# Where the gate of w_out is multiplied in: from the weights to the output projection's product

## The chip, the cores and the metric

The kernel runs on one core of a Trainium2 chip. Five engines of that core matter here: TensorE (PE in the profile; PEld is its loading of weights), VectorE (DVE), ScalarE (ACT), GpSimd (POOL) and SyncE (SP), which issues nearly all DMA transfers. Each engine works off its own queue in order, and instructions of different engines wait for each other on semaphores. The metric is the device time of one execution in microseconds (us).

## The reference, cut to what matters

One layer of a diffusion backbone works on a sequence of 2048 latent tokens of 1024 channels (`x`). Six vectors of 1024 numbers come from the conditioning vector `c`; one of them, `g1`, is the gate of the first residual addition:

```
h = modulate(rmsnorm(x, norm_mix), sh1, sc1)
o = token_mixers(h @ w_in, ...)          # (2048, 1024): recurrence heads and gMLP heads
x = x + g1 * (o @ w_out)                 # the output projection, gated, added
h2 = modulate(rmsnorm(x, norm_ffn), sh2, sc2)
x = x + g2 * conv_ffn(h2, w_up, conv_w, conv_b, w_down)
out = rmsnorm(x, norm_final)
```

`g1` has one number for each of the 1024 output columns. So `g1 * (o @ w_out)` is the same as `o @ (w_out * g1)`, with the columns of `w_out` scaled.

## The kernel before, in words

**Matmuls in three parts.** Every large product is made of float32r matmuls. An operand is split into a rounded high part and the rest (`split`, L131: a cast on ACT, L133, and a subtraction, L134, on the engine that is passed, POOL if none), and `mm3` (L136) adds up high by high, high by low and low by high. In the profile L65 is every matmul, L69 every transpose on TensorE.

**Two halves of the sequence, heads in turn.** The first and longest part (to about 978 us) runs the input projection for the two halves of 1024 tokens. `run_banks` (L524) walks over blocks of 128 columns of `w_in`; each block's weights are loaded into one of three raw tiles of 4 KB per partition (`raw_tile`, L214) and split by ACT and DVE. Between the blocks' matmuls the work of the recurrence is spread out: `hg` (L791) for one head and half, with sums over columns of `kh` and `kl` (L798, L800), levels of scores and `mi` banks for transposes and states; `sgu` (L678) for the gMLP heads, with the normalised tile `nt` (L709).

**Due times.** This spread-out work consists of Python generators in two lists, `hg_q` and `bg_q`. `slot()` (L185) is called after every three matmuls; a generator goes on once the modelled time of TensorE has advanced by the number that it last yielded, in us. So `yield 5.0` in a background step means: the next piece is put into the queues 5.0 us of matmul time later. Behind that a planner orders the instructions of each engine, by when it reckons that each can start; instructions under `pin` stay in the program's order.

**w_out in the background.** `w_out_ops` (L982) is one generator of `bg_q`, between the blocks that make the six vectors (`ada_block`, L951, which also stores `g1` and `g2` in `g_d`) and the taps and `w_down_ops` (L999). For each of the 8 blocks of 128 rows and each of the 2 halves of 512 columns it takes a raw tile, loads the half row into its left half (L989) and the gate, broadcast to 128 partitions, into its right half (L990); 5.0 us later it multiplies on DVE (L993), splits into `wo_hi` and the tile's right half (L994), stores both into `wo_d` (L995, L996), and 2.5 us later begins the next. `wo_hi` has the tag `acc`, with one buffer. `w_down_ops` loads whole raw tiles (L1007), multiplies them by `g2` 9.0 us later (L1009) and stores them (L1010).

**The output projection.** From 978 to 1168 us, `wo` is in SBUF (13 loads, L916 and L1145) and TensorE works through 16 tiles of 128 tokens (L1334). For tile t the code asks for tile t+2's operand (`fetch_o`, L1317) and tile t+1's rows of `x` (`fetch_x`, L1327), splits tile t+1's operand (`split_o`), and multiplies into `pd`, a PSUM tile of two banks of 512 columns, first the one bank, then the other (48 matmuls). There are two such tiles in turn. DVE adds the rows of `x` (L1358, giving `xn`), SP stores `xn` (L1359), and ACT squares it and sums the squares (L1360). After every second tile `second_norm` (L1275) makes the reciprocal roots on POOL (L126, L128), scales the two tiles on DVE (L1279), and then, in four steps, transposes them on TensorE, applies `a2` and `s2` (L1292) and splits the result (L1295 to L1305). Its transposes are put into the queue as background: the first `first` = 6.0 us of matmul time behind the pair's end, the others 3.0 us apart. For the last pair these are 9.0 and 4.5.

**Then** the up-projection, the convolution and the down-projection follow, to the end of the span. `a_tiles` (L1196) gives the split weights of the up-projection; its tags `Ah` and `Al` have four buffers each, of 2 KB per partition, and three of the four pairs are filled while the output projection ends.

Of the kernel before, what the change touches and what calls it, by code (L numbers as in the profile page):

```python
# [9 lines left out]
F32 = mybir.dt.float32  # L10
F32R = mybir.dt.float32r
# [7 lines left out]
P = 128  # L19
# [14 lines left out]
AL = 512  # L34
# [49 lines left out]
def tile_trunk(ctx, tc, x, c, cx, c_ctx, w_ada, b_ada, norm_mix, norm_ffn, w_in, hg_norm, sgu_g, sgu_b,  # L84
               w_sp, b_sp, w_out, w_up, conv_w, conv_b, w_down, norm_final, masks, out):
    nc = tc.nc
    V, S, G, T = nc.vector, nc.scalar, nc.gpsimd, Tensor(nc.tensor)
    ld = nc.sync.dma_start
    st = nc.sync.dma_start
# [3 lines left out]
    w_ada, w_in, w_out, w_up, w_down = w_ada[0], w_in[0], w_out[0], w_up[0], w_down[0]  # L93
# [21 lines left out]
    g_d = dr.tile([2, D], F32, name="g_d")  # L115
# [3 lines left out]
    wo_d = dr.tile([P, NK, 2, D], F32, name="wo_d")  # L119
# [11 lines left out]
    def split(hi, lo, raw, eng=None, keep=lambda i: i):  # L131

        keep(S.copy(hi, raw))  # L133
        (eng or G).tensor_sub(lo, raw, hi.bitcast(F32))  # L134

    def mm3(ps, lhi, llo, rhi, rlo, first, last):  # L136
        T.matmul(ps, lhi, rhi, start=first, stop=False)
        T.matmul(ps, lhi, rlo, start=False, stop=False)
        T.matmul(ps, llo, rhi, start=False, stop=last)
# [51 lines left out]
    with es1:  # L191
# [22 lines left out]
        def raw_tile():  # L214
            return p1.tile([P, D], F32, tag="raw", name="raw", bufs=3)
# [766 lines left out]
        def w_out_ops():  # L982

            for k in range(NK):
                for n in range(2):
                    cl = slice(n * 512, n * 512 + 512)
                    raw = raw_tile()
                    w, g = raw[:, :512], raw[:, 512:]
                    ld(w, w_out[k * P:(k + 1) * P, cl])  # L989
                    ld(g, g_d[0:1, cl].broadcast_to([P, 512]))  # L990
                    yield 5.0
                    hi = pm.tile([P, 512], F32, tag="acc", name="wo_hi")
                    V.tensor_mul(w, w, g)  # L993
                    split(hi.bitcast(F32R), g.bitcast(F32R), w, V)  # L994
                    st(wo_d[:, k, 0, cl], hi)  # L995
                    st(wo_d[:, k, 1, cl], g)  # L996
                    yield 2.5

        def w_down_ops():  # L999

# [174 lines left out]
    px = esx.enter_context(tc.tile_pool(name="px", bufs=1, reuse_waits="tile"))  # L1175
# [10 lines left out]
    def zbank():  # L1186
        return ps2.tile([P, 512], F32, tag="uz", name="uz", bufs=2)
# [5 lines left out]
    def dbank():  # L1193
        return ps2.tile([P, 2, 512], F32, tag="dn", name="dn", bufs=2)
# [4 lines left out]
    def v_tile():  # L1199
        return px.tile([P, TH + GW], F32, tag="cv", name="cv", bufs=3)  # L1200
# [4 lines left out]
    def raw_tile2(j):  # L1205
        return px.tile([P, 4, 2 * P], F32, tag=f"raw{j}", name="raw")


    class Unit:
# [15 lines left out]
        def prep(self, i):  # L1225

            a11, a21 = self.raw[0][:, :, :P], self.raw[0][:, :, P:]
            a12, a22 = (self.raw[1][:, :, :P], self.raw[1][:, :, P:]) if i else (None, None)
            self.A[i] = a_tiles()
            hi, lo = self.A[i]  # L1230

            if i == 1:
                self.s2 = (c_tile()[:, :4, :].bitcast(F32) if self.slots[0] == 1 else
                           px.tile([P, 4, P], F32, tag="s1", name="s2"))
            split(hi, lo, (a11, a12, self.s2, a11, a21, a12, a22)[i])
            if i == 0:
                G.tensor_sub(a21, a11, a21)
            elif i == 1:
                pin(G.tensor_sub(self.s2, a22, a21))
            elif i == 2:  # L1240
                G.tensor_add(a11, self.s2, a11)
            elif i == 3:
                G.tensor_sub(a12, a12, self.s2)  # L1243
# [30 lines left out]
    with tc.tile_pool(name="po", bufs=1, reuse_waits="tile") as po:  # L1274
# [39 lines left out]
        def fetch_o(t):  # L1314
            hh, g = tiles[t]
            raw = raw_tile2(2 * (t % 2 == 0)).rearrange("p a b -> p (a b)").rearrange("p (k c) -> p k c", c=P)
            ld(raw, oT_d[hh][:, :, g * P:(g + 1) * P])  # L1317
            return raw

        def split_o(t, raw):  # L1320
            o = po.tile([P, 2, NK, P], F32R, tag="o", name="o", align_bytes=AL) if t % 2 else first_o[0]()
            split(o[:, 0], o[:, 1], raw, V, pin)
            return o

        def fetch_x(t):
            xt = raw_tile2(2 if t == nt_ - 1 else 1 + 2 * (t % 2))
            ld(xt.rearrange("p a b -> p (a b)"), x[t * P:(t + 1) * P, :])  # L1327
            return xt.rearrange("p a b -> p (a b)")

        raw_o = {1: fetch_o(1)}  # L1330
        xts = {0: fetch_x(0)}
        ops = {0: first_o[1]}
        xs = []
        for t, (hh, g) in enumerate(tiles):  # L1334
            if g % 2 == 0:
                ss = px.tile([P, 2], F32, tag="ss", name="ss", bufs=2)
            if t + 2 < nt_:
                raw_o[t + 2] = fetch_o(t + 2)
            if t + 1 < nt_:
                ops[t + 1] = split_o(t + 1, raw_o.pop(t + 1))  # L1340
                xts[t + 1] = fetch_x(t + 1)
            if t + 2 == nt_:
                units[0].load()
            if t + 1 == nt_:
                units[1].load_half(0)
            pd = dbank()
            o = ops.pop(t)
            for n in range(2):
                for k in range(NK):
                    mm3(pd[:, n, :], o[:, 0, k, :], o[:, 1, k, :], wo[k][:, 0, n * 512:(n + 1) * 512],  # L1350
                        wo[k][:, 1, n * 512:(n + 1) * 512], k == 0, k == NK - 1)
                    if t + 1 < nt_ or n == 0 and k < 4:
                        bg_q.slot()
            if t + 1 == nt_:
                for n in range(3):
                    prep(n)
            xn = v_tile()[:, :D]
            V.tensor_add(xn, pd.rearrange("p a b -> p (a b)"), xts.pop(t))  # L1358
            st(xn_d[t], xn)  # L1359
            S.activation(pd.rearrange("p a b -> p (a b)"), xn, AF.Square, accum_out=ss[:, g % 2:g % 2 + 1])  # L1360
            if t + 1 == nt_:
                units[1].load_half(1)
            xs.append(xn)
            if g % 2:
                how = (ubank, 6.0, 3.0) if t + 1 < nt_ else (lambda: dbank()[:, 0, :], 9.0, 4.5)
                norm = second_norm(hh, g - 1, xs, ss, *how)
                if t + 1 < nt_:
                    bg_q.drain()
                wait = next(norm)
                bg_q.drain()  # L1370
                bg_q.add(norm)
                bg_q.at = T.t + wait
                xs = []
# [193 lines left out]
    for n, (u, i) in enumerate(prods):  # L1567
# [10 lines left out]
        p = zbank() if i == 1 else u.z if i in (4, 6) else u.x  # L1578
        hi, lo = u.A[i]
# [40 lines left out]
    V = Kept(nc.vector, pin)  # L1620
# [111 lines left out]
    xts, odd_ss = {}, {}  # L1732
# [131 lines left out]
```

## Time and profile before

| | before |
|---|---|
| median of 3 runs | 2441.85 us (2439.68 to 2443.75) |
| the profiled execution | 2441.35 us, span 2439.6 us |
| TensorE busy | 2403.6 us (99% of the span) |
| DVE / ACT / POOL busy | 1669.5 / 1039.4 / 882.7 us |
| moved by SP's queue | 397.28 MB |
| 368 to 504 us, where w_out is rounded: TensorE / DVE / ACT busy of 136 | 131.58 / 83.00 / 60.81 us |
| 978 to 1168 us, the output projection: TensorE / DVE / ACT busy of 190 | 188.70 / 104.71 / 86.07 us |

How it is read: a row of the profile's groups names the line, the engine, the operation, what is written and read (`out<-in`), the shapes and the count; behind the bar stand the busy time, the mean duration in ns, and the time that the engine stood idle just before these instructions, with what ended most of it. In a timeline a row has the start, the duration, and in brackets the idle time before it. A table of stretches gives each engine's busy time (with the instructions), the clock that TensorE was granted as a share of full speed, the share of the DMA engines' time and the GB/s.

### The profile page before, as it was taken

The numbers are of one execution on the slowest core, as the hardware profiler recorded it, in microseconds if no ns is written. First come the engines' busy times: TensorE is split into PE (matmuls) and PEld (weight loads), VectorE is DVE, ScalarE is ACT, GpSimd is POOL, SyncE is SP. The second block draws the span as 40 slices with busy tenths as digits, with TensorE's granted clock in tenths as the row PEclk, the third lists the DMA queues.
The fourth block names the chain that finished last, engine by engine and source line by source line (L and its number), as shares of the span: only waits on it lengthen the run. The fifth ranks groups of instructions, "written<-read, shape, count | busy, mean of one in ns | idle before, by whom it ended". The sixth has DMA issues, their size and how long they took to land.

```text
span 2439.6 us, 32382 instructions
## 1 busy us (share of the span) xinstructions
PE 2403.6 (99%) x11711; PEld 1995.0 (82%) x11711; DVE 1669.5 (68%) x2293; ACT 1039.4 (43%) x1802; POOL 882.7 (36%) x796
## 2 busy tenths in 40 slices
PE   8999999999999999999999999999999999999998
PEld 5887887888888887788888888888888887888887
DVE  5867795756776786465596666639866772776875
ACT  4554334434444443354554444434445442332343
POOL 1232110110121132000688778787888870000002
PEclk9999999999999999999999999999999999999999
DMA  8365446573354323768922322562222238934745
GB/s 311 108 209 163 152 136 196 193 241 121 113 177 156 104 104 141 239 209 260 309 82 86 97 81 91 183 230 97 86 94 86 88 112 334 324 121 147 229 153 196
DMA packets 307853, 400.10 MB, mean 164 GB/s; under 512 B 33113, under 2 KB 216161, under 8 KB 304621
## 3 DMA queue, kind: packets, MB, share of 16 engines
q1 hardware_dynamic: 304404, 397.28, 48.3%
q8 instruction: 92, 1.51, 0.2%
q10 hardware_dynamic: 3289, 0.76, 0.1%
q14 instruction: 68, 0.56, 0.1%
HBM read 288.85 MB, written 109.13 MB: 163 GB/s over the span
## 4 chain that ended last, share of the span: by engine, by line
PE 47%; issue 2%; POOL 1%; DVE 1%; ACT 1%; SPq 0%; DMA 0%; POOLq 0%; ACTq 0%
PE ux L65 19%; PE uz L65 14%; PE dn L65 14%; POOL ra L1723 0%; POOL rr L1724 0%; DVE dn L1434 0%; POOL Al L134 0%; ACT mhl L133 0%; ACT jk L1715 0%; DVE odd L80 0%; ACT odd L1793 0%; DVE mhl L80 0%; DVE thl L80 0%; ACT thl L133 0%; POOL raw L1243 0%
## 5 line engine op out<-in xcount | busy, mean ns | idle before, releaser
L1434 DVE SCALAR_TENSOR_TENSOR dn<-gp,taps,dn 128x1024 f32<-128x1024 f32 x352 | 448.3, 1285 | 97.2 <-ACT dn L1431 92.8
L65 PE MATMUL dn<-thl,mhl 128*128 128x512 f32 x1680 | 381.5, 389 | 1.2 <-ACT thl L133 1.2
L65 PEld LDWEIGHTS dn<-thl,mhl 128*128 128x128 f32 x1680 | 315.1, 188 | 67.6 <-ACT thl L133 2.1
L134 POOL TENSOR_TENSOR Al<-raw,Ah 128x512 fp32r<-128x512 f32 x264 | 341.3, 1309 | 69.3 <-ACT Ah L133 40.5
L65 PE MATMUL pj<-xh,whi 128*128 128x512 f32 x896 | 362.4, 405 | 0.0
L65 PE MATMUL pj<-xl,whi 128*128 128x512 f32 x896 | 351.3, 392 | 0.6 <-POOL xl L134 0.6
L65 PE MATMUL pj<-xh,wlo 128*128 128x512 f32 x896 | 350.9, 392 | 0.9 <-DVE wlo L134 0.9
L133 ACT CAST Ah<-raw 128x512 fp32r<-128x512 f32 x264 | 163.0, 620 | 240.4 <-PE ux L65 134.6
L65 PE MATMUL ux<-xah,Ah 128*128 128x512 f32 x528 | 205.7, 390 | 0.3 <-ACT keep L1498 0.3
L65 PEld LDWEIGHTS pj<-xh,wlo 128*128 128x128 f32 x896 | 168.4, 188 | 36.9 <-DVE wlo L134 1.1
L65 PEld LDWEIGHTS pj<-xh,whi 128*128 128x128 f32 x896 | 168.9, 189 | 33.7 <-issue 3.5
L65 PEld LDWEIGHTS pj<-xl,whi 128*128 128x128 f32 x896 | 169.1, 189 | 31.9 <-POOL xl L134 1.5
L65 PE MATMUL dn<-wo,o 128*128 128x512 f32 x768 | 182.9, 394 | 1.7 <-DVE nt L717 0.9
L65 PE MATMUL uz<-yf,Ah 128*128 128x512 f32 x704 | 174.0, 389 | 0.0
L590 POOL TENSOR_TENSOR K<-K,tot 128x512 f32<-128x512 f32 x40 | 58.3, 1458 | 303.8 <-DVE tot L520 158.0
L65 PEld LDWEIGHTS dn<-wo,o 128*128 128x128 f32 x768 | 142.0, 188 | 31.6 <-issue 1.1
L65 PE MATMUL ux<-yf,Ah 128*128 128x512 f32 x528 | 155.4, 389 | 0.0
L65 PEld LDWEIGHTS uz<-yf,Ah 128*128 128x128 f32 x704 | 132.1, 188 | 27.4
L65 PE MATMUL ux<-xah,Al 128*128 128x512 f32 x528 | 141.7, 390 | 1.0 <-POOL Al L134 1.0
L65 PE MATMUL ux<-xal,Ah 128*128 128x512 f32 x352 | 137.1, 389 | 0.0
L1723 POOL TENSOR_SCALAR ra<-ss 128x1 f32<-128x1 f32 x8 | 5.3, 662 | 360.4 <-ACT jk L1715 360.4
L134 DVE TENSOR_TENSOR wlo<-raw,whi 128x1024 fp32r<-128x1024 f32 x68 | 85.1, 1252 | 72.6 <-ACT whi L133 70.7
(345 smaller groups left out, 4480.5 us busy)
## 6 DMA issues: line engine op xcount, KB each, us to landing
raw<-in_w_up_dram SPq DMA_DIRECT2D x88, 512.0 KB
mr<-m SPq DMA_DIRECT2D x85, 512.0 KB
raw<-in_w_in_dram SPq DMA_DIRECT2D x68, 512.0 KB
sT<-wd SPq DMA_DIRECT2D x88, 256.0 KB
raw<-in_w_ada_dram SPq DMA_DIRECT2D x32, 512.0 KB
yf<-yd SPq DMA_DIRECT2D x14, 1024.0 KB
m<-cv SPq DMA_DIRECT2D x22, 544.0 KB
raw<-in_w_down_dram SPq DMA_DIRECT2D x22, 512.0 KB
```

The costliest lines, as they stand in the source:

```text
L65: return self.engine.matmul(out, lhsT, rhs, **kw)
L133: keep(S.copy(hi, raw))
L134: (eng or G).tensor_sub(lo, raw, hi.bitcast(F32))
L590: e.tensor_mul(view(K2, row * W + o, src), view(K, o, src), view(tot, t0, [[4, n], [ts, 2], [0, B]]))
L1434: V.scalar_tensor_tensor(out=cr, in0=gt[:, t // 3:t // 3 + RH, t % 3:t % 3 + GW], scalar=taps[:, t * NF + f:t * NF + f + 1], in1=cr, op0=A ...
L1723: G.tensor_scalar(out=a, in0=ss, scalar1=plus, scalar2=None, op0=ALU.add)
```

## The change

The gate leaves the weights. `w_out_ops` loads a whole row block of 1024 columns into the raw tile (one load of 512 KB in place of two of 256 KB), without the gate; it waits 9.0 us in place of 5.0, splits the first half into `wo_hi` and, in place, the rest, and the second half 4.0 us later; the low parts of both halves are stored by one transfer. In the output projection the two halves of the gate are loaded once into a buffer of `Ah` and one of `Al`, broadcast to 128 partitions, and DVE multiplies each half of the product by its half of the gate into `xn` and then adds the rows of `x` in SBUF.

```diff
         def w_out_ops():
 
             for k in range(NK):
+                raw = raw_tile()
+                ld(raw, w_out[k * P:(k + 1) * P, :])
+                yield 9.0
                 for n in range(2):
                     cl = slice(n * 512, n * 512 + 512)
-                    raw = raw_tile()
-                    w, g = raw[:, :512], raw[:, 512:]
-                    ld(w, w_out[k * P:(k + 1) * P, cl])
-                    ld(g, g_d[0:1, cl].broadcast_to([P, 512]))
-                    yield 5.0
                     hi = pm.tile([P, 512], F32, tag="acc", name="wo_hi")
-                    V.tensor_mul(w, w, g)
-                    split(hi.bitcast(F32R), g.bitcast(F32R), w, V)
+                    split(hi.bitcast(F32R), raw[:, cl].bitcast(F32R), raw[:, cl], V)
                     st(wo_d[:, k, 0, cl], hi)
-                    st(wo_d[:, k, 1, cl], g)
-                    yield 2.5
+                    if n == 0:
+                        yield 4.0
+                st(wo_d[:, k, 1, :], raw)
+                yield 2.5
...
         raw_o = {1: fetch_o(1)}
         xts = {0: fetch_x(0)}
+        gate = []
+        for n, w in enumerate(("Ah", "Al")):
+            gate.append(px.tile([P, 512], F32, tag=w, name=f"gate{n}", bufs=4, align_bytes=AL))
+            ld(gate[n], g_d[0:1, n * 512:n * 512 + 512].broadcast_to([P, 512]))
         ops = {0: first_o[1]}
...
             xn = v_tile()[:, :D]
-            V.tensor_add(xn, pd.rearrange("p a b -> p (a b)"), xts.pop(t))
+            for n in range(2):
+                V.tensor_mul(xn[:, n * 512:n * 512 + 512], pd[:, n, :], gate[n])
+            V.tensor_add(xn, xn, xts.pop(t))
             st(xn_d[t], xn)
```

## The prediction

> **What bounds the kernel now.** I read the page's totals first, then the chain of waits for TensorE, then the two stretches that the change touches: 368 to 504 us, where w_out is rounded, and 978 to 1168 us, the output projection.
>
> ```profile
> span 2439.6 us, 32382 instructions
> PE 2403.6 (99%) x11711; PEld 1995.0 (82%) x11711; DVE 1669.5 (68%) x2293; ACT 1039.4 (43%) x1802; POOL 882.7 (36%) x796
> ```
>
> TensorE is busy for 2403.6 of 2439.6 us. So a change pays only where it closes a gap of TensorE, and costs only where it opens one; DVE, ACT and DMA time by itself is free. The profiled execution took 2441.35 us, 1.75 us more than its span and 0.5 us less than the median of the runs, 2441.85. I sum against the span and carry the difference over to the median.
>
> TensorE's waits from 365 to 520 us (total, times, longest), all there are:
>
> ```profile
> PE mi L69 <- DVE nt L709: 1.6, 1, 1.6
> PE sc L65 <- ACT kh L798: 1.5, 1, 1.5
> PE sc L65 <- DVE kl L800: 1.3, 1, 1.3
> ```
>
> **Part 1: w_out's rounding.** It loses 16 multiplies by the gate and 16 loads of the gate row (8 loads of whole rows stand for 16 of halves), and a row is now rounded 9.0 us of matmul time behind its request and not 5.0. The groups by line, for the multiply of before in its stretch, and for w_down's multiply, whose code already asks for a whole tile 9.0 us ahead (the last number is DVE's idle time just before them):
>
> ```profile
> L993 DVE TENSOR_TENSOR raw<-raw 128x512 f32<-128x512 f32 x16 | 11.0, 689 | 29.8 <-DMA raw<-g_d 29.8
> L1009 DVE TENSOR_TENSOR raw<-raw,g 128x1024 f32<-128x1024 f32 x22 | 27.9, 1267 | 0.0
> ```
>
> DVE stood 29.8 us in front of multiplies whose gate had not landed, with everything behind them in its queue; at 9.0 us it never waited. So 11.0 us of multiplies and 29.8 us of DVE blocking go. What that is worth is two places. In order of time:
>
> ```profile
> 402.25 0.42 SPq L990 DMA_DIRECT2D raw<-g_d  x1
> 406.25 0.69 DVE L993 TENSOR_TENSOR raw<-raw 128x512 f32<-128x512 f32 x1 [3.12 <-DMA raw<-g_d]
> 408.49 0.59 ACT L566 ACTIVATE F<-pj 128x512 f32<-128x512 f32 x1
> 409.76 1.22 DVE L794 TENSOR_TENSOR Q<-K 128x1024 f32<-128x1024 f32 x1
> 411.94 1.22 DVE L795 TENSOR_TENSOR Q<-Q,qs 128x1024 f32<-128x1024 f32 x1
> 413.19 1.04 ACT L798 CAST kh<-Q 128x1024 fp32r<-128x1024 f32 x1 [3.59 <-DVE Q L795]
> 414.29 0.50 PE L65 MATMUL sc<-kh,ones_r 128*128 128x512 f32 x1 [1.50 <-ACT kh L798]
> ...
> 465.72 0.69 DVE L993 TENSOR_TENSOR raw<-raw 128x512 f32<-128x512 f32 x1 [2.74 <-DMA raw<-g_d]
> 470.65 1.36 DVE L709 TENSOR_SCALAR nt<-mi,mv,rs 128x128 f32<-128x128 f32 x4 [1.41 <-POOL rs L128]
> 472.07 0.66 PE L69 MATMUL mi<-ident,K 128*128 128x128 f32 x4 [1.64 <-DVE nt L709]
> ```
>
> A 3.12 us stall of DVE at 406 pushes the rounding casts, the gate activations, L794, L795 and the cast of kh back, and TensorE waits 1.5 and then 1.3 us for the two halves. A 2.74 us stall at 465 does the same to nt, 1.6 us. Both stalls are longer than the TensorE waits behind them, so with the cover of 9.0 us these 4.4 us should go. The first place has a price beyond its gaps; stretches with TensorE's busy time, granted clock, DMA share and GB/s:
>
> ```profile
> 414.00:417.00 3.00, 1.43 (x3) 0.81 0.48 178
> 417.00:419.50 2.50, 2.50 (x8) 0.55 0.16 62
> 419.50:422.00 2.50, 2.50 (x13) 1.00 0.32 108
> ...
> 472.10:474.60 2.50, 2.50 (x13) 1.00 0.66 222
> ```
>
> Behind the two gaps 8 matmuls ran in 2.5 us at a clock of 0.55 where 13 run otherwise: five matmuls of 0.19 us, 1.0 us more. The gap of 1.64 us at 472 cost no clock. In all 4.4 + 1.0 = 5.4 us can go. I take 4.5, because the remaining casts and subtractions land at other moments and one wait of about 0.9 us may appear. Ends: 5.4 at best, 0 at worst.
>
> The Trainium skill, "TensorE: Matmul & The Clock Gate", Part 1, says that the clock halves after an idle window of about 3.4 us. By that rule neither gap would have cost clock and the gain would be 4.4 at most; the row with 0.55 behind gaps of 1.5 and 1.3 us says otherwise, and I go by the row.
>
> What the new order adds here: the second half of a row is rounded only 4.0 us behind the first, and wo_hi has one buffer (tag acc), which is free again when its store has landed:
>
> ```profile
> 379.37 0.32 SPq L995 DMA_DIRECT2D wo_d<-wo_hi  x1
> 382.88 0.62 ACT L133 CAST wo_hi<-raw 128x512 fp32r<-128x512 f32 x1 [1.23 <-DMA wo_d<-wo_hi]
> ```
>
> That store took 3.5 us from its issue until ACT went on. A cast of 0.62, then 3.5, is 4.1 us against a distance of 4.0 plus the rounding to the next slot: just covered, and where SP is late ACT waits a microsecond or so with its evictions behind it, eight times at most. This is the 0.9 that I keep back, and a rival below. The low-half store now carries a whole row, after the second half, so a raw buffer is held about 13 us; w_down holds one for 9.0 plus its multiply and store in the same pool of three with no DVE wait, so I cost that at nothing. SP issues 32 DMAs here in place of 64. Eight steps of 9.0 + 4.0 + 2.5 take 124 us, sixteen of 7.5 took 120; later background work moves by a few slots: 1.5 us either way, 0 in the sum.
>
> **Part 2: the output projection.** L1358, one addition of 128x1024, becomes two multiplies of 128x512 and an addition of 128x1024. A pair of tiles, in order of time:
>
> ```profile
> 1025.18 1.22 DVE L1358 TENSOR_TENSOR cv<-dn,raw 128x1024 f32<-128x1024 f32 x1 [0.35 <-PE dn L65]
> 1026.44 1.03 ACT L1360 ACTIVATE dn<-cv 128x1024 f32<-128x1024 f32 x1 [2.45 <-DVE cv L1358]
> 1028.75 0.75 DVE L1279 TENSOR_SCALAR cv<-cv,rs 128x1024 f32<-128x1024 f32 x1 [2.35 <-POOL rs L128]
> 1029.42 1.22 DVE L134 TENSOR_TENSOR o<-raw,o 128x1024 fp32r<-128x1024 f32 x1
> 1030.55 0.74 DVE L1279 TENSOR_SCALAR cv<-cv,rs 128x1024 f32<-128x1024 f32 x1
> 1031.10 0.80 PE L69 MATMUL ux<-ident,cv 128*128 128x128 f32 x4
> ```
>
> Addition, square, root on POOL, two scalings: every step waits for the one before, and the transposes stand in TensorE's queue 6.0 us behind the tile's end. Is there slack? Of the waits on L1279:
>
> ```profile
>   PEld ux L69: 2.9, 7
> ```
>
> None: in all seven pairs that are followed by a tile the weight load of these transposes already waits. Whatever is put into the chain, TensorE pays, seven times. How much: the multiply of the second half can start only at the tile's end and takes 0.69 (L993's mean, same shape). The first half's product is complete half a tile earlier; whether its multiply then runs depends on the planner, which does move this step by readiness:
>
> ```profile
> 1013.29 1.22 DVE L1358 TENSOR_TENSOR cv<-dn,raw 128x1024 f32<-128x1024 f32 x1
> 1014.43 0.28 DVE L1296 TENSOR_TENSOR fl<-fl 128x128 f32<-128x128 f32 x1
> ```
>
> L1296 stands ahead in the program and yet runs behind. So I take 0.7 us a pair, 7 x 0.7 = 4.9; with both multiplies behind the tile's end 2 x 0.69 x 7 = 9.7; the lower end is under Rivals. The even tiles' additions feed no wait of TensorE. The last pair has cover on POOL:
>
> ```profile
> 1172.56 0.19 ACT L1360 ACTIVATION_READ_ACCUMULATOR dn<-cv 128x1 f32 x1
> 1173.62 1.30 POOL L134 TENSOR_TENSOR Al<-s,Ah 128x512 fp32r<-128x512 f32 x1
> 1175.00 0.19 POOL L126 TENSOR_SCALAR rs<-ss 128x2 f32<-128x2 f32 x1
> ```
>
> The sum is ready at 1172.75 and POOL free at 1174.92: 2.2 us, more than 1.4. Nothing there.
>
> The two gate loads (0.52 MB) enter SP's queue as the stage opens, and one Ah and one Al buffer each stay taken through it; the fourth weight split, which needs them back, comes after the last product. DMA is full there:
>
> ```profile
> 966.00:989.00 23.00, 22.07 (x107) 18.11 (x105) 7.38 (x26) 3.04 (x4) 5.99 (x6) 1.00 1.03 362
> 988.21 1.05 ACT L133 CAST o<-raw 128x1024 fp32r<-128x1024 f32 x1 [11.46 <-DMA raw<-oT]
> ```
>
> In the program they stand behind tile 1's operand, for which ACT waits until 988.21, and ahead only of loads that are needed a tile later: nothing. If the planner issues them first, 0.52 MB at 362 GB/s delay that operand, and TensorE, by 1.4 us. I take 0.
>
> **Sum.** -4.5 + 4.9 + 0 + 0 = +0.4 on the span: 2440.0, or 2442.3 on the median. 0.2% of it, 4.9 us, is about what a measurement of this kernel can tell from no change.
>
> **Rivals.**
> A, the planner lets the next tile's matmuls run ahead of the transposes. It does so elsewhere:
>
> ```profile
> 327.13 0.50 PE L65 MATMUL sc<-knh,ones_r 128*128 128x512 f32 x1
> 327.47 0.40 PE L65 MATMUL pj<-xh,whi 128*128 128x512 f32 x1
> ```
>
> The column sums are consecutive in the program. Against it: in the seven pairs it left the transposes where the program has them, though they wait. A pair would then cost about 0.2 (a switch of operand shape costs 0.1 here: 0.34 us from 327.13 to the next start against 0.23 between equal matmuls), 1.4 in all: -4.5 + 1.4 = -3.1, 2438.8.
> B, slower: both multiplies run behind the tile's end, 0.69 a pair more. It decides once a pair loses more than 1.34 us: -4.5 + 9.7 = +5.2, 2447.1. For it: two half products of one tile, which may be waited for as one. Against it: DVE is idle for almost half of the stage.
> C, ACT waits for the store of wo_hi and the gaps at 414 and 472 stay: +4.9, 2446.8. The Trainium skill, "DMA: Bandwidth & Descriptors", Anatomy of one DMA, puts the fixed part at about 2 us, with which the buffer would be back in time; the row of 3.5 us makes it close.
> D, the clock is cut behind each pair's gap as it was behind 414: 7 x 1.0 more, +7.4, 2449.3. The gap of 1.64 us at 472, with the clock at 1.00 behind it, speaks against it.
> E, the whole 5.4 goes, a pair costs 0.1 and the shift of w_down brings 1.5: -6.2, 2435.7.
>
> **Chances.** Forecast 0.42, A 0.23, B 0.19, C 0.06, D 0.03, E 0.07. The range leaves out most of E and the far end of D: 2437.0 to 2449.0. Faster by over 0.2%: E and a tail of A, 0.12. Slower: half of B and more, half of C, D, and the upper tail of the forecast where the gate loads come first, 0.26. Within: 0.62.
>
> **What would show it.** After: no DVE wait on a gate in w_out's stretch; no TensorE wait for kh, kl or nt there above 0.5 us and a clock of 1.00; in the output projection a TensorE wait of about 0.7 us before each pair's transposes; DVE busy near 1669.5 - 11.0 + 32 x 0.69 = 1680.6. Wrong would be: transposes with more than 27 matmuls of the tile ahead of them (A), 1.4 us waits (B), waits of wo_hi for its store with TensorE behind them (C).

## The result, and the profile after

The changed kernel takes 2456.45 us in the median of its runs (2455.2 to 2459.62), against 2441.85 before: a ratio of 1.0061, 95% interval 1.0049 to 1.0073. It is slower by 14.6 us, where +0.4 was forecast. The profiled execution took 2455.2 us. The totals of its page:

```profile
span 2453.4 us, 32368 instructions
PE 2403.9 (98%) x11711; PEld 1992.1 (81%) x11711; DVE 1683.6 (69%) x2309; ACT 1039.2 (42%) x1802; POOL 882.0 (36%) x796
```

TensorE did the same work in 13.8 us more, and it was busy for 0.3 us more (stretches at a slower clock come in both traces and about even out): over the whole span the loss is gaps. To see where they lie, compare the two traces at the same matmul of TensorE's queue. The table has the start of a matmul after, less its start before; the second column takes off the 0.31 us by which the traces differ already at 343 us, ahead of everything that the change touches.

| matmul | after - before | less 0.31 | gained or lost since the row above |
|---|---|---|---|
| first product of the output projection | -6.16 | -6.47 | -6.47: w_out's rounding |
| first product of its third tile | -5.06 | -5.37 | +1.09: the projection's first two tiles |
| first matmul of the up-projection | +0.95 | +0.64 | +6.01: seven pairs |
| its 49th | +8.38 | +8.07 | +7.43: the step behind the last pair |
| its 301st | +9.22 | +8.91 | +0.84 |
| first of the down-projection | +9.22 | +8.91 | 0 |
| its 145th | +14.01 | +13.70 | +4.79 |
| end of the span | +13.85 | +13.54 | -0.16 |

**w_out's rounding.** TensorE's waits from 365 to 520 us after the change, all of them, and a stretch around the matmuls of kh (busy time of TensorE, its weight loads, DVE, ACT and POOL, each with the instructions; then the granted clock, the DMA share and the GB/s):

```profile
PE mi L69 <- DVE nt L709: 0.5, 1, 0.5
```
```profile
413.00:415.50 2.50, 2.39 (x11) 1.67 (x10) 2.50 (x4) 1.24 (x3) 0.00 (x0) 1.00 0.28 105
```

The waits for kh and kl and the stretch with a clock of 0.55 are gone; 0.5 of the 1.6 us for nt is left. That is 3.9 us of waits. The trace of before has the clock at half for 3.4 us from 415.9 us, which is worth up to 1.7 us more; the prediction counted 1.0 of it.

**A pair.** DVE in order of time around the end of an odd tile, before and then after, and TensorE after (start, duration, idle time ahead in brackets):

```profile
1047.94 0.55 DVE L134 TENSOR_TENSOR fl<-fl,yst 128x384 fp32r<-128x384 f32 x1
1049.06 1.23 DVE L1358 TENSOR_TENSOR cv<-dn,raw 128x1024 f32<-128x1024 f32 x1 [0.57 <-PE dn L65]
1052.64 0.75 DVE L1279 TENSOR_SCALAR cv<-cv,rs 128x1024 f32<-128x1024 f32 x1 [2.35 <-POOL rs L128]
...
1054.44 0.75 DVE L1279 TENSOR_SCALAR cv<-cv,rs 128x1024 f32<-128x1024 f32 x1
```
```profile
1046.26 0.55 DVE L134 TENSOR_TENSOR fl<-fl,yst 128x384 fp32r<-128x384 f32 x1
1046.73 1.28 DVE L1362 TENSOR_TENSOR cv<-dn,gate 128x512 f32<-128x512 f32 x2
1048.04 1.22 DVE L1363 TENSOR_TENSOR cv<-cv,raw 128x1024 f32<-128x1024 f32 x1
...
1053.42 0.75 DVE L1278 TENSOR_SCALAR cv<-cv,rs 128x1024 f32<-128x1024 f32 x1
```
```profile
1052.52 0.30 PE L69 MATMUL ux<-ident,cv 128*128 128x128 f32 x1 [0.96 <-DVE cv L1278]
1052.58 1.87 PE L65 MATMUL dn<-wo,o 128*128 128x512 f32 x7
1054.29 0.49 PE L69 MATMUL ux<-ident,cv 128*128 128x128 f32 x3
```

Both multiplications start behind the tile's whole product, here and in all 16 tiles, and the first transpose waits 0.96 us. Before, DVE stood idle for 0.57 us until the product ended; after, it comes straight from the previous pair's arithmetic (no bracket).

**Behind the last pair.** Tile 14's addition, the up-projection's weights that are loaded into the buffer of its x rows, and the scaling of the last pair, before and after:

```profile
1158.58 1.22 DVE L1358 TENSOR_TENSOR cv<-dn,raw 128x1024 f32<-128x1024 f32 x1
1160.21 0.43 SPq L1218 DMA_DIRECT2D raw<-in_w_up_dram  x1
1176.02 1.42 DVE L1279 TENSOR_SCALAR cv<-cv,rs 128x1024 f32<-128x1024 f32 x2 [5.15 <-POOL rs L128]
```
```profile
1161.55 1.22 DVE L1363 TENSOR_TENSOR cv<-cv,raw 128x1024 f32<-128x1024 f32 x1
1164.22 0.67 SPq L1364 DMA_DIRECT2D xn<-cv  x1
1164.94 0.45 SPq L1217 DMA_DIRECT2D raw<-in_w_up_dram  x1
1181.03 0.19 POOL L126 TENSOR_SCALAR rs<-ss 128x2 f32<-128x2 f32 x1
1182.05 3.42 DVE L1278 TENSOR_SCALAR cv<-cv,rs 128x1024 f32<-128x1024 f32 x2 [8.12 <-POOL rs L128]
1183.86 0.33 PE L69 MATMUL dn<-ident,cv 128*128 128x128 f32 x1 [1.94 <-DVE cv L1278]
1185.53 0.69 PE L69 MATMUL dn<-ident,cv 128*128 128x128 f32 x2 [1.34 <-DVE cv L1278]
```

Tile 14's addition ends 3.0 us later, and the load that may only then overwrite the x rows is issued 4.7 us later, behind the store of `xn` in SP's queue. POOL, which splits these weights, then waits for it:

```profile
POOL raw L1236 <- DMA raw<-in_w_up_dram: 14.5, 1, 14.5
```

So POOL reaches the reciprocal root (L126) at 1181.03 in place of 1175.00, and the transposes, in TensorE's queue, wait for the scaling behind it. TensorE's waits in this step are 1.66 us for ACT's copy of an up-projection product (it stands in ACT's queue behind a cast that waits for POOL), and the 1.94 and 1.34 us above: 4.9 in all. Behind them TensorE's clock was granted at half for 3.4 us:

```profile
1185.50:1188.90 3.40, 3.37 (x10) 2.80 (x11) 3.37 (x4) 0.00 (x0) 2.53 (x2) 0.50 0.00 0
1188.90:1192.30 3.40, 3.40 (x17) 2.72 (x15) 1.17 (x2) 2.50 (x4) 1.70 (x2) 1.00 0.44 134
```

Half of 3.4 us is up to 1.7 us more. Waits and clock together make up to 6.6 of the 7.4 us.

**The down-projection's start.** SP's and TensorE's waits from 2010 to 2070 us after, and TensorE's one wait there before:

```profile
SPq L1657 <- PE dn L65: 11.5, 1, 11.5
...
PE dn L65 <- ACT thl L133: 3.3, 2, 2.7
```
```profile
PE dn L65 <- ACT thl L133: 0.8, 1, 0.8
```

SP holds the first load of `sS` (rows of the second half, kept in SBUF for the down-projection) for 11.5 us until matmuls are done, with all later loads behind it. Before, SP had no such wait. The clock takes its part here too: it was granted at 0.50 from 2045.7 to 2049.1 us, up to 1.7 of the 4.8 us.

### The profile page after: what moved, and what is told of

The parts are those of the page before. It is cut to its first block, busy times and chain, and to the rows that moved or that the text cites. A ratio compares the mean times of both kernels' runs of the same rounds, so it can differ in the third digit from the quotient of the medians.

```text
span 2453.4 us, 32368 instructions
## 1 busy us (share of the span) xinstructions
PE 2403.9 (98%) x11711; PEld 1992.1 (81%) x11711; DVE 1683.6 (69%) x2309; ACT 1039.2 (42%) x1802; POOL 882.0 (36%) x796
## 4 chain that ended last, share of the span: by engine, by line
PE 46%; issue 2%; POOL 1%; DMA 1%; DVE 1%; ACT 1%; SPq 0%; POOLq 0%; ACTq 0%; DVEq 0%
PE ux L65 19%; PE uz L65 14%; PE dn L65 13%; POOL Al L134 0%; DMA mr<-m 0%; POOL ra L1728 0%; DMA sT<-wd 0%; POOL rr L1729 0%; ACT mhl L133 0%; DMA yd<-fl 0%; DVE dn L1439 0%; ACT jk L1720 0%; DVE odd L80 0%; POOL s L1238 0%; ACT odd L1798 0%
## 5 line engine op out<-in xcount | busy, mean ns | idle before, releaser
L134 POOL TENSOR_TENSOR Al<-raw,Ah 128x512 fp32r<-128x512 f32 x264 | 340.7, 1306 | 70.1 <-ACT Ah L133 39.1
L134 DVE TENSOR_TENSOR wlo<-raw,whi 128x1024 fp32r<-128x1024 f32 x68 | 85.1, 1252 | 90.2 <-ACT whi L133 89.2
```

## The experiments

Each kernel's ratio is to the kernel before, on the same chip, with its 95% interval. Their traces are read like the table above, each less its own difference at 343 us. A row is one traced execution, and executions of one kernel differ by up to 8.9 us (2441.34 to 2450.24 for the gate by halves), so a row's sum and its ratio can differ by a few us:

| kernel | ratio | first product | to the third tile | seven pairs | last step | 49th to 301st | down-projection |
|---|---|---|---|---|---|---|---|
| changed | 1.0061 (1.0049 to 1.0073) | -6.47 | +1.09 | +6.01 | +7.43 | +0.84 | +4.79 |
| part 1 alone | 0.9973 (0.9964 to 0.9983) | -6.41 | +0.89 | -0.26 | 0.00 | +0.03 | -0.01 |
| its rows, multiplied | 0.9971 (0.9960 to 0.9983) | -5.62 | +0.45 | -0.30 | 0.00 | +0.10 | -0.07 |
| longer distance only | 1.0013 (1.0004 to 1.0022) | +3.12 | +2.52 | +0.21 | 0.00 | -0.03 | -0.01 |
| gate by halves, DVE | 1.0003 (0.9994 to 1.0013) | -1.55 | +1.56 | -0.33 | 0.00 | +0.37 | 0.00 |
| the same, one multiplication | 1.0012 (1.0003 to 1.0021) | +1.74 | -0.38 | +0.39 | 0.00 | -0.21 | 0.00 |
| gate by halves, POOL | 1.0021 (1.0013 to 1.0030) | +4.40 | +0.80 | -0.09 | 0.00 | +0.26 | -0.04 |
| loads as before, POOL | 1.0037 (1.0025 to 1.0050) | +12.20 | +0.02 | -0.52 | 0.00 | +0.25 | -0.04 |
| part 2 alone | 1.0076 (1.0059 to 1.0093) | +1.25 | +0.01 | +7.88 | +6.21 | +2.08 | +4.35 |
| gate buffers only | 1.0020 (1.0011 to 1.0030) | -0.66 | -0.06 | -0.23 | 0.00 | -0.27 | +4.59 |
| buffers placed late | 1.0042 (1.0027 to 1.0057) | -6.55 | +0.95 | +6.07 | +7.62 | +1.01 | 0.00 |
| last pair plain | 1.0022 (1.0012 to 1.0032) | -6.59 | +2.83 | +6.49 | 0.00 | +1.33 | +4.72 |
| tile 14 plain | 1.0024 (1.0015 to 1.0034) | -6.52 | +1.23 | +7.49 | +0.13 | +2.47 | +3.95 |
| late, tile 14's rows elsewhere | 1.0013 (1.0004 to 1.0021) | -6.37 | +0.67 | +6.20 | +1.56 | +2.35 | -0.01 |
| late, even tiles gated | 1.0009 (1.0000 to 1.0018) | -8.15 | +3.43 | +4.26 | +6.71 | +0.95 | -0.04 |
| late, odd tiles gated | 1.0008 (0.9999 to 1.0017) | -8.16 | +3.27 | +5.77 | +1.20 | +1.10 | +0.25 |
| first half early | 1.0083 (1.0068 to 1.0098) | -6.59 | +8.56 | +10.09 | +5.80 | +2.52 | +4.33 |
| late, transposes later | 1.0027 (1.0017 to 1.0037) | -8.01 | +3.69 | +8.02 | +2.28 | +5.78 | -0.44 |
| late, rows elsewhere, transposes later | 1.0041 (1.0028 to 1.0054) | -8.20 | +1.25 | +10.10 | +2.33 | +5.99 | -0.44 |

Part of the scatter is the clock, granted at half for 3.4 us at a time, up to 1.7 us of work each. The six rows with 2.5 us or more to the third tile have such a stretch between 983 and 1002 us (two in a row in "first half early"), the others have none; so that column is read no finer than this. Up to 1.7 us of the last step is clock with the buffers placed late, as in the changed kernel, and of the pairs in the last three rows; of the column 49th to 301st it is up to 3.4 in the last two. In the first column, two kernels whose code up to there is that of before (part 2 alone, gate buffers only) differ from before by +1.25 and -0.66, so nothing under about 1 us is read there.

**The parts apart.** Part 1 alone is the kernel before with the changed `w_out_ops` and no gate at all; part 2 alone has the old `w_out_ops` and the changed projection.

> Part 1 alone: w_out's rows whole, no gate on the weights, and no gate anywhere else either (the output leaves the attention branch's gate out). If the trace of the changed kernel is read rightly, the first product matmul of the attention projection starts 6.2 us earlier than before and nothing is given back later: -6 us, about 2436. The prediction's term was -4.5 with an end at -5.4: about 2437. If the 6.2 us came from anything else than part 1, no change.

> Part 2 alone: the weights gated and rounded as before, and the product multiplied as well (so the gate is applied twice). Theory: pairs +6.0, the step after the last pair +7.4, POOL's low halves +1.3, the start of the down-projection +4.8, start of the projection +1: about +20 us, 2462. The prediction's terms: +4.9 (its ends 1.4 to 9.7). If the losses exist only because the projection starts 6 us earlier (gate and weights loads then collide with others), much less than +20: about +8.

Part 1 alone gains 0.27%, and behind the third tile nothing is given back. Part 2 alone loses in the same four places as the changed kernel, although its projection starts no earlier. So the losses come from part 2 and not from an earlier start. The 1.09 us at the first two tiles is not a price of the gate's loads: part 1 alone, without them, has 0.89.

**The place of the gate's buffers.** The first kernel only adds to the kernel before the lines that ask for the two gate buffers and load them; nobody reads them. The second is the changed kernel with the stage's other tags asked for first:

```diff
+        px.tile([P, 2], F32, tag="ss", name="ss", bufs=2)
+        raw_tile2(2)
+        raw_tile2(3)
+        v_tile()
+        px.tile([P, 8], F32, tag="rs", name="rs")
+        px.tile([P, 8], F32, tag="rs2", name="rs2")
+        c_tile()
+        px.tile([P, 7, P], F32R, tag="yst", name="yst", bufs=2, align_bytes=AL)
         gate = []
         for n, w in enumerate(("Ah", "Al")):
```

> The kernel before with the two gate buffers asked for and loaded where the changed kernel does it, and never read: output and all other work as before. Placement theory: pairs and last pair as before, +4.8 us at the start of the down-projection, about +5 in all, 2446.5; and up to +1 at the projection's start if the two loads delay the second tile's operand. Rival (lateness from the up-projection): 0.

> The changed kernel with the other buffers of the stage asked for ahead of the gate's, so that the weights' split buffers (whose slots the gate borrows) keep the place in SBUF that they had before; nothing else. Placement theory: the wait of SP's queue for the first sS load at the start of the down-projection goes, and with it 4.8 us: about 2451.5, +9.5 on before. Rival (the down-projection's loads are late because the up-projection ends 9 us later, or its queue is fuller): no change to the changed kernel, +14.5 on before.

Waits from 2010 to 2070 us: SP's and TensorE's with the gate buffers only, and SP's first entry for the same line in the kernel with the buffers placed late:

```profile
SPq L1656 <- PE dn L65: 11.5, 1, 11.5
...
PE dn L65 <- ACT thl L133: 4.6, 2, 2.5
```
```profile
SPq L1665 <- DMA sS<-m: 7.9, 9, 0.9
```

Both went as the placement theory said. Two unread buffers bring SP's 11.5 us wait and +4.59 us (here by longer waits of TensorE, with the clock at 1.00); with the order of first asking restored the wait is gone and the loss is 0.00. That is what follows if a tag gets its place in SBUF when it is first asked for: asked for at the opening of the stage, `Ah` and `Al` lie where `sS` is put later, and `sS` must wait for the first down-projection matmuls, which still read split weights from these buffers. The runs show the order of asking as the cause; the places themselves were not read out.

**The last step.** Two kernels leave the gate out of the addition for tiles 14 and 15 (the diff), and for tile 14 alone (`t != nt_ - 2` in its condition):

```diff
-            for n in range(2):
-                V.tensor_mul(xn[:, n * 512:n * 512 + 512], pd[:, n, :], gate[n])
-            V.tensor_add(xn, xn, xts.pop(t))
+            if t < nt_ - 2:
+                for n in range(2):
+                    V.tensor_mul(xn[:, n * 512:n * 512 + 512], pd[:, n, :], gate[n])
+                V.tensor_add(xn, xn, xts.pop(t))
+            else:
+                V.tensor_add(xn, pd.rearrange("p a b -> p (a b)"), xts.pop(t))
```

> The changed kernel with the last two tiles' products added to x without the gate (these 256 rows leave the gate out). Theory: the step from the projection to the up-projection loses 7.4 us in the changed kernel because tile 14's addition, and so the release of its x rows' buffer for the first weights, comes late; here most of it goes: about -7 on the changed kernel, +7.5 on before. The prediction's step (nothing to be lost behind the last pair): no change to the changed kernel, +14.5.

> The changed kernel with tile 14 alone added without the gate (128 rows leave it out); tile 15 keeps both multiplications behind the last product. If the loss comes from tile 14's x rows (the weights' buffer), -5.5 to -6.5 on the changed kernel. If it comes from tile 15's own multiplications on the way to the last transposes, no more than -1.

The step falls from +7.43 to 0.00, and with tile 14 alone plain to +0.13. Tile 15's own multiplications, which stand right on the way to the last transposes, cost 0.13 us; tile 14's cost the rest, through the buffer of its x rows. (In the whole time tile 14 alone recovers less than its 7.3: the pairs and the low halves behind it cost 3.1 more there.) The cause can also be taken away with every product gated, by loading tile 14's rows into the buffer of its sum and multiplying in PSUM:

```diff
+            if t == nt_ - 2:
+                xt = v_tile()[:, :D]
+                ld(xt, x[t * P:(t + 1) * P, :])
+                return xt
...
+            prod = pd.rearrange("p a b -> p (a b)") if t == nt_ - 2 else xn
             for n in range(2):
-                V.tensor_mul(xn[:, n * 512:n * 512 + 512], pd[:, n, :], gate[n])
-            V.tensor_add(xn, xn, xts.pop(t))
+                V.tensor_mul(prod[:, n * 512:n * 512 + 512], pd[:, n, :], gate[n])
+            V.tensor_add(xn, prod, xt)
```

> The changed kernel with the gate's buffers placed late (as in the run before) and tile 14's x rows loaded into the buffer of its sum, so that the first weights of the up-projection wait for no addition; all products gated. Theory: the 7.4 us of the step after the last pair go, nothing else: about +2 on before (the placed-late kernel had +9). Rival (tile 15's multiplications or POOL's work hold that step as well): +6 to +9.

The step costs 1.56 in place of 7.62, and 1.3 us more are lost in the matmuls behind it. Of the kernels with the gate on every product this is the best, and still 0.13% slower than before.

**The pairs.** First the prediction's assumption: the first half's multiplication is written behind the first half's products.

```diff
+                if n == 0:
+                    xn = v_tile()[:, :D]
+                    V.tensor_mul(xn[:, :512], pd[:, 0, :], gate[0])
```

> The changed kernel with the first half's multiplication written behind the first half's products, ahead of the second half's. If it then runs during the second half (the prediction's assumption), each pair loses about 0.45 in place of 0.86 us and the step after the last pair about 1 us less: -3 to -4 on the changed kernel, about 2452.5. If VectorE's queue puts it off or the loss isn't in the chain from the product to the transposes: no change.

TensorE's waits in it from 985 to 1182 us:

```profile
PE dn L65 <- ACT o L133: 7.2, 3, 6.6
PE ux L69 <- DVE cv L1278: 5.9, 7, 1.6
PE dn L65 <- DVE o L134: 2.4, 5, 0.6
PE dn L65 <- DVE cv L1359: 1.7, 2, 1.0
```

It is slower by another 0.2%. The multiplication (L1359) does run ahead of the tile's end, and the waits for the scaling stay (5.9; in the changed kernel 5.5). New ones join them: TensorE waits for L1359 itself, and for the next tile's operand, whose low half (L134) goes through the same queue of DVE; the 6.6 us stall is at the second tile's operand, and why the planner's order there runs into it I did not follow. Next, each kind of tile alone, on the kernel with the buffers placed late. The edit is that of tiles 14 and 15 with another condition, here for the even tiles; for the odd ones it asks for 1:

```diff
-            if t < nt_ - 2:
+            if t % 2 == 0:
```

> The changed kernel with the gate's buffers placed late, and the second tile of each pair (the odd ones) added without the gate (half the rows leave it out). If a pair's 0.86 us is the 1.4 us that the second tile's multiplications add between its last product and the scaling the transposes wait for, the loss from the projection's second tile to its last falls from 6.1 us to 1 or less. If it is the even tile's multiplications standing in VectorE's queue among the pair before, 3 us or more stay. The step after the last pair keeps its loss (tile 14 is gated).

> The changed kernel with the gate's buffers placed late and the first tile of each pair (the even ones) added without the gate (half the rows leave it out). With the even tiles' multiplications alone the pairs kept 0.7 us each. If the odd tile's multiplications cost as much by themselves (they stand between its last product and the scaling), 4 us or more stay between the projection's third tile and its last. If they are free without the even ones, 1 or less. Tile 14 is not gated here, so the step after the last pair loses less than 1 us either way.

DVE around the end of the same odd tile (tile 5) with even tiles gated, and with odd tiles gated:

```profile
1047.21 0.55 DVE L134 TENSOR_TENSOR fl<-fl,yst 128x384 fp32r<-128x384 f32 x1
1047.68 1.22 DVE L1374 TENSOR_TENSOR cv<-dn,raw 128x1024 f32<-128x1024 f32 x1
...
1053.05 0.75 DVE L1278 TENSOR_SCALAR cv<-cv,rs 128x1024 f32<-128x1024 f32 x1
```
```profile
1043.41 0.55 DVE L134 TENSOR_TENSOR fl<-fl,yst 128x384 fp32r<-128x384 f32 x1
1044.46 1.29 DVE L1371 TENSOR_TENSOR cv<-dn,gate 128x512 f32<-128x512 f32 x2 [0.50 <-PE dn L65]
1045.78 1.23 DVE L1372 TENSOR_TENSOR cv<-cv,raw 128x1024 f32<-128x1024 f32 x1
...
1051.16 0.75 DVE L1278 TENSOR_SCALAR cv<-cv,rs 128x1024 f32<-128x1024 f32 x1
```

Neither kind is free, and they don't add: 4.26 and 5.77 alone, 6.07 together. With odd tiles gated, DVE idles 0.50 us until the product ends, as before, and the chain behind it is longer by the multiplications. With even tiles gated the chain is as short as before, but DVE reaches the addition straight from the arithmetic on the previous pair's columns, which the even tile's multiplications had pushed back; the 0.5 us of slack are eaten, and the addition begins late. With both, the last scaling of the median pair ends 8.9 us behind the next tile's first matmul (7.2 with even tiles alone, 7.7 with odd ones, 6.3 before), and yet a pair costs hardly more. The count of the next tile's matmuls ahead of the transposes suggests why: 27 ahead of all four before, and with even tiles gated in five of the seven pairs, where the planner moved nothing; 27 ahead of the first and 30 to 36 ahead of the other three with odd tiles gated, 30 to 38 with both. The planner gave three of four transposes more room, and what TensorE pays is mostly the first one, which it left where it was.

**A later due time for the transposes** (`first` 8.0 in place of 6.0 for the pairs), on the kernel with the buffers placed late, without and with tile 14's rows elsewhere:

> The changed kernel with the gate's buffers placed late and each pair's first transpose due 8.0 in place of 6.0 us behind its scaling in the planner's time. If the pairs' loss is TensorE reaching a transpose that its queue holds too early, most of the 0.86 us a pair (6 in all) goes: about +3 on before. If VectorE's added work itself holds the chain (other operands late too), the waits move to the next products: no change, +9.

> Both edits together, with the buffers placed late. If the three losses are separate, what stays is part 1's gain less about 1 us at the projection's first tiles and 1.3 us at the low halves: -3 to -4 on before, about 2438.5. If they hide one another, +1 or more.

TensorE's waits from 985 to 1210 us in the second of the two:

```profile
PE ux L69 <- DVE cv L1278: 8.7, 7, 2.9
PE ux L65 <- ACT Ah L133: 5.0, 1, 5.0
...
```

The edits don't add up: the waits for the scaling are larger in sum (8.7 us, against 5.7 with the buffers placed late), and the up-projection's first weights are late. The first pairs do get cheaper (0.7 us each or less up to the tenth tile, against 0.6 to 1.1), but what is put off piles up at the last tiles. All four transposes now stand behind 36 matmuls in place of 27, and TensorE still waits for the scaling: the chain itself ends later. Both theories failed here; the planner re-orders more than the one step that was moved, and what delays the chain was not followed further.

**What in part 1 brings the gain.** The longer distance alone is the kernel before with `yield 9.0` in place of `yield 5.0`. The multiplied rows are part 1 alone with one line more:

```diff
                     hi = pm.tile([P, 512], F32, tag="acc", name="wo_hi")
+                    V.tensor_mul(raw[:, cl], raw[:, cl], raw[:, cl])
```

> The kernel before with one number changed: the half rows of w_out and their gate are multiplied and rounded 9 us behind their request in place of 5. If VectorE's waits for these transfers (29.8 us in the kernel before) are what TensorE loses its 6 us to, -5 to -6 on before, about 2437. If it is VectorE's multiplications (11.0 us), 0 to -1.

> Part 1 alone (whole rows, no gate's load, 9 us behind the request) with the 16 multiplications put back on VectorE, each half row by itself in place, so that no second operand has to come (the output leaves the gate out and squares the weights). Against part 1 alone this adds 11 us of VectorE and nothing else. If the gate's loads were what cost TensorE its 6 us, -5 to -6 on before stays. If it is the multiplications and where they stand in VectorE's queue, 0 to -2 is left or less.

With the multiplications back on DVE and no gate to load, the gain stays: 0.9971. DVE's 11 us cost TensorE 0.8 us at the first product (-5.62 against -6.41), which is within that column's scatter, and nothing in the ratio. With the longer distance alone DVE waited for the gate as much as before; TensorE no longer waits for kh and kl, but longer for nt, with the clock at half for 3.4 us behind that wait, and at 521 us the kernel is only 0.5 us ahead. It loses 3.2 us behind 878 us. Waits from 343 to 530 us (DVE) and 360 to 600 us (TensorE), and then w_down's multiplications, before and here (durations, first and last start):

```profile
DVE raw L993 <- DMA raw<-g_d: 31.6, 8, 7.4
...
PE mi L69 <- DVE nt L709: 3.2, 1, 3.2
```
```profile
L1009 DVE TENSOR_TENSOR raw<-raw,g x22: 1209/1217/2314, 544.8 to 831.9; 128x1024 f32<-128x1024 f32 x22
```
```profile
L1009 DVE TENSOR_TENSOR raw<-raw,g x22: 1207/1215/2311, 615.8 to 915.7; 128x1024 f32<-128x1024 f32 x22
```

Sixteen steps of 11.5 us take 64 us longer than sixteen of 7.5, and w_down's last multiplications now stand among the last heads, where TensorE has new waits for kl (1.6 us at 882) and knl (1.1 at 892).

So at an unchanged number of loads the distance buys little here, and makes the background late. That leaves the gate's loads, with what went along with them: whole rows, 32 transfers in place of 64, and other steps. But loading each half of the gate once, with the gate still on the weights, did not keep the gain either:

```diff
+            for n in range(2):
+                gt = pm.tile([P, 512], F32, tag="acc", name="go")
+                ld(gt, g_d[0:1, cl].broadcast_to([P, 512]))
+                for k in range(0, NK, 2):
+                    raw = raw_tile().rearrange("p (a c) -> p a c", a=2)
+                    ld(raw, w_out[k * P:(k + 2) * P, cl].rearrange("(a p) c -> p a c", p=P))
+                    yield 9.0
+                    for i in range(2):
+                        w = raw[:, i, :]
+                        hi = pm.tile([P, 512], F32, tag="ot", name="wo_hi", bufs=2)
+                        V.tensor_mul(w, w, gt)
+                        split(hi.bitcast(F32R), w.bitcast(F32R), w, V)
...
```

The second kernel multiplies the two rows at once and splits them 2.0 us later; in the third GpSimd does the two multiplications, 4.0 us ahead of the splits; the fourth has the loads of the kernel before, with GpSimd multiplying:

> The gate stays on the weights, but each half of it is loaded once, two rows of blocks of the half lie in one buffer, and they are multiplied and rounded 9 us behind their request; the projection is as before. If it is the waits for the gate's and weights' transfers that part 1 removed, nearly all of its gain is here: -5.5 to -6 us, about 2436. If it is the 11 us of multiplications on VectorE that counted, no more than -2.

> The gate on the weights by halves, one multiplication for two rows of blocks, 2 us ahead of the rounding, so that ScalarE's copy doesn't wait for VectorE. If the halves' version lost its gain to that wait (3.2 us in ScalarE's queue ahead of the next head's weights), -5 on before, 2437. If VectorE's 10 us of multiplications cost it anyway: 0 to -2.

> The gate on the weights by halves, multiplied by GpSimd instead of VectorE (16 multiplications of a 128x512 tile), projection as before. If VectorE's multiplications are what the halves' versions still paid, -5 to -6 on before, as with part 1 alone. If the order in which the planner puts the rounding among the heads' work decides, anything from -6 to +2, with other waits than in the run on VectorE.

> The kernel before's loads (half rows, with their gate each), but multiplied by GpSimd 6 us behind the request and rounded 2 us later. Multiplications and waits both gone from VectorE: -5 to -6 on before. If the planner's order decides: -6 to +2.

In the first of these DVE's wait for the gate is down to 1.0 us, and TensorE, from 360 to 600 us, has other waits, the longest of which are:

```profile
DVE raw L995 <- DMA go<-g_d: 1.0, 1, 1.0
```
```profile
PE pj L65 <- ACT whi L133: 1.6, 1, 1.6
PE pj L65 <- DVE wlo L134: 0.8, 1, 0.8
...
```

The whi and wlo are the next block's weights, which here are split too late. The version with one multiplication has its own such waits, and with POOL multiplying, ACT's casts wait for POOL instead. So the multiplications are not what part 1 gains by. The gate's loads go with the gain, but to load them once is not enough: the versions that do so differ from part 1 also in their steps and in the planner's order, and no run parts these. What decides stays open. No kernel that computes the gated layer came out faster than the one before.

## Why the prediction was wrong, step by step

**Part 1** (-4.5, ends 0 and -5.4): right in place, sign and mechanism of the waits; -5.4 from the third tile on, at its best end. "At 9.0 us it never waited" was the wrong half of the reason: with the distance alone DVE waited on (31.6 us), and the gain came only where the gate's loads went as well. The cover of the `wo_hi` store did not hold: from 365 to 520 us ACT waited for it six times, 8.9 us in all and up to 3.4 at once (before: three times, 4.8 us). Yet TensorE's 0.5 us for nt is all that is left there, so rival C's first sign came and its price did not. The shift of w_down was worth nothing, as assumed (its last multiplication starts at 826.9 us against 831.9); the longer distance alone shows what it costs when it is 84 us.

**The pairs** (4.9, ends 1.4 and 9.7): 6.0, a term mis-sized by 1.1, and near by luck. The assumption behind it fell: no first half was multiplied early, which is rival B's mechanism; and written early it cost more. Rival B's price (9.7) was too high in turn. Part of the 1.37 us was slack: 0.5 us of DVE idling per pair. That 1.37 less 0.5 is so close to the measured 0.86 proves little, since the planner also moved three transposes of four and the even and odd tiles' costs don't add. "The even tiles' additions feed no wait of TensorE" is refuted by the even tiles alone, 4.26 us. Rival A came for three transposes of four (30 to 38 matmuls ahead of them, where more than 27 was its sign), and the one that stayed keeps the wait. Rival D did not come between the pairs (a clock of 1.00 from 983 to 1168 us), but its mechanism did in two places where the prediction had no gap, behind the last pair and at the down-projection's start.

**The last pair** ("2.2 us, more than 1.4. Nothing there"): this step failed, by 7.4 us, of which up to 1.7 are the clock behind the waits. It took POOL's row at 1175.00 as fixed. POOL's time is set by the arrival of the weights, this by the release of tile 14's x rows, and this by the very instruction that the change lengthens. The two kernels with tile 14 plain, and the one with its rows elsewhere, show it.

**The gate's loads** (0): right. **The gate's buffers** ("the fourth weight split comes after the last product", cost nothing): right for the up-projection but for 0.8 us at its low halves, and blind to what the early request does to the place of two tags, 4.8 us in a stage that the prediction did not name. With 7.4 this is nearly all of the miss, as the traces have it: 0.4 - 0.9 + 1.1 + 7.4 + 0.8 + 4.8 = 13.6, against 13.5 measured.

Of the signs named beforehand, no wait on a gate, no wait above 0.5 us in w_out's stretch and the clock of 1.00 came true, and the waits before the pairs' transposes, 5.5 us in eight up to 1168 us, were near the 0.7 us each; DVE busy was 1683.6 against 1680.6.

## What to carry to other kernels

When an instruction gets longer, ask besides its chain what it releases: a buffer freed later can hold the next stage's first load, and that load's consumer may be the engine that was counted as cover. A buffer asked for earlier can move others in SBUF and make a far stage wait; compare the queue of transfers at the start of each later stage, and restore the order of first asking where it matters. And an engine that is idle almost half of a stage still has no slack if it takes its work in order and a chain passes through it twice: each of two additions may cost nearly as much as both. Price a gap of the bottleneck by more than its length: behind two of the gaps here its clock was cut as well.

## What the runs showed of the hardware

DVE slowed down beside POOL. The last pair's two scalings took 1.42 us together before (1176.02), while POOL stood still, and 3.42 after (1182.05), when POOL was at work on weights all the while. POOL, before and after:

```profile
1177.92 1.32 POOL L134 TENSOR_TENSOR Al<-raw,Ah 128x512 fp32r<-128x512 f32 x1 [1.93 <-ACT Ah L133]
```
```profile
1181.99 1.26 POOL L134 TENSOR_TENSOR Al<-raw,Ah 128x512 fp32r<-128x512 f32 x1
1183.21 1.71 POOL L1238 TENSOR_TENSOR fl<-raw 128x512 f32<-128x512 f32 x1
```

The same in the addition of the last tile, which before read PSUM and SBUF and now reads SBUF twice, before and after:

```profile
1169.09 1.23 DVE L1358 TENSOR_TENSOR cv<-dn,raw 128x1024 f32<-128x1024 f32 x1 [2.67 <-PE uz L69]
```
```profile
1171.36 2.11 DVE L1363 TENSOR_TENSOR cv<-cv,raw 128x1024 f32<-128x1024 f32 x1
```

So up to 2.0 of the 7.4 us, by an estimate from these rows, were two engines in each other's way, on top of the lateness that brought them together. The Trainium skill, "GPSIMD Engine Reference", section 1 (Specifications), says that GpSimd's interfaces to SBUF are shared with VectorE and contend with its instructions with two SBUF inputs or in a mode that uses two ports; for the addition with two SBUF inputs the rows agree, 2.11 us beside POOL against 1.22 for tile 14's. No run measured that cost by itself.

TensorE's clock. In every trace here the stretches at half clock between 343 us and the last matmuls are 3.4 us long, or twice that. The length of one gap did not decide whether one came. At the down-projection's start the changed kernel had waits of 2.69 and 0.23 us with the clock at 0.50 behind them; with the gate buffers only they were 2.52 and 0.22 us, and the clock stayed at 1.00. Before, 1.50 and 1.28 us at 414 us were enough, and 1.64 us at 472 us was not. What decides was not tested.
